# Transposing softmax tiles in 32x32 blocks on VectorE and placing the blocks by DMA over DRAM, in a two-layer attention trunk

## The chip, the cores and the metric

The kernel runs on one core of a Trainium2 chip. The metric is the device time of one execution in microseconds (us); 2468.92 us is the median of three runs of the kernel before (2468.75 to 2469.18). The trace was taken in one more execution on the same kind of chip.

## The reference

The reference is a two-layer encoder on 256 tokens of 2048 features, in float32. Each layer is a mixer and a gated feed-forward network (FFN, 5632 wide, with a convolution of width 3 on the gate), each behind an RMS norm and with a residual sum. Four kinds of attention heads make up the two mixers; in all of them a softmax over keys is multiplied with the values:

```python
# layer 0, A: 8 heads, three dilated windows each, merged by their softmax denominators
logits = einsum("bqhd,bqkhd->bhqk", qi, kg) * scale + rel_bias        # per (window, dilation)
o = einsum("bhqk,bqkhd->bqhd", exp(logits - m), vg) / denom
out_a = sum(softmax(stack(lses), axis=0)[..., None] * stack(outs), axis=0)
# layer 0, B: 4 heads, two softmax maps each
w = p[:, :, 0] - lam * p[:, :, 1];  o = einsum("bhqk,bkhd->bqhd", w, v)   # then a norm per head
# layer 1, C: 8 heads that share 2 key/value heads, with rotary q and k
o = einsum("bngqk,bknd->bqngd", softmax(logits), v)
# layer 1, D: 8 heads, a clamped 2-D neighbourhood with a learned bias
o = einsum("bhjrc,brjchd->bjhd", softmax(logits), vq)
```

Each mixer ends in an output projection of its concatenated heads. The output is the RMS norm of the last residual.

## The kernel before

Nearly all the work is projections, whose weights are read from DRAM once, in units of 128x1024 float32 (512 KB). For each unit SyncE starts a load into one of five `raw` buffers; ScalarE casts it to float32r (`wh`, line 230) and VectorE takes the rest (`wl = raw - wh`, line 233); there are four buffers of each. TensorE multiplies high by high, high by low and low by high parts. `gemm_b` (line 141) makes transposed results for queries, keys and the FFN: for two 128-wide results it runs four units' high products (line 132), then their low ones (line 138). `gemm_a` (line 198) makes row-wise results of 512 columns, a unit being 12 products (lines 194 to 196).

Attention work is put between the projections by a clock written out by hand. `tick()` (line 85) moves the clock on; `gemm_b` ticks twice (for queries and keys once between its high and low products and once behind them), `gemm_a` behind every second unit. `later(delay, fn, rank)` (line 81) queues a step for the tick `delay` ahead; in one tick steps of lower rank come first. `flush()` ticks until nothing is queued. The framework's planner then orders each engine's instructions by when it reckons them ready, except where `keep_in_program_order` pins one, and makes each wait only for what it needs and for its buffer to be released.

A head's steps are: queries and keys; two ticks later the logits (TensorE, then VectorE adds the bias into `sc` or `scc`) and the softmax (`softmax`, line 414, `b_softmax`, line 652, or `c_head`, line 818); two ticks later the transposes of the probabilities and their split into a high and a low part, `pt` (`transposed_probs`, line 393, `a_transposes`, line 570); then the products with the values: one tick later in A and B heads (`a_values`, `b_values`), two in C and D heads (`head_out`, line 402). B heads have one step more, `b_finish` (line 694). TensorE transposes 128x128 float32 blocks by a product with the identity, into PSUM tiles `tp` (`transpose_block`, line 273). An A head's softmax tile is 128x1024: per half of the queries 256 columns of the local window and 128 of each strided one. The other heads' tiles are 128x512. `sc` has one buffer; `scc` has two.

There are 28 heads: 8 A, 4 B, 8 C and 8 D. The A and B heads start one per three or two `gemm_b` calls, a C head one per tick, a D head one per `gemm_b`. `mixer_out` (line 326) is the output projection: it runs seven of eight units of its first two chunks with ticks, flushes, and then multiplies the last units, which need the last two head outputs (`mix`).

GpSimd does little: it loads bias rows (lines 538 and 545), runs of D's bias table (line 867) with a sum (line 871), and small constants, each through its own DMA queue.

Of the kernel before, what the change touches and what calls it, by code (L numbers as in the profile page):

```python
# [27 lines left out]
F32 = mybir.dt.float32  # L28
F32R = mybir.dt.float32r
AF = mybir.ActivationFunctionType  # L30
ALU = mybir.AluOpType
AX = mybir.AxisListType

P = 128
SEQ = 256
# [11 lines left out]
NACT = 24  # L47
RAW = 5
AHEAD = 4


def rev(ap):
# [6 lines left out]
def trunk_kernel(ctx: ExitStack, tc, a, out):  # L59
# [13 lines left out]
    def nm(s):  # L73
        uid[0] += 1
        return f"{s}_{uid[0]}"
# [5 lines left out]
    def later(delay, fn, rank=2):  # L81

        pending.append((now[0] + delay, rank, fn))
# [19 lines left out]
    def tps(tag, bufs):  # L103
        return psum.tile([P, 512], F32, name=nm(tag), tag=tag, bufs=bufs)
# [22 lines left out]
    def two(ap):  # L127
        return ap.rearrange("p (a b) -> p a b", a=2)
# [100 lines left out]
    def split(dst_h, dst_l, src, pin=False):  # L229
        first = S.copy(dst_h, src)  # L230
        if pin:
            tc.keep_in_program_order(first)
        V.tensor_tensor(dst_l, src, dst_h.bitcast(F32), op=ALU.subtract)  # L233
# [39 lines left out]
    def transpose_block(pairs):  # L273

        for i, (dst, src) in enumerate(pairs):
            ins = T.transpose(dst, src, ident)  # L276
            if i:
                tc.keep_in_program_order(ins)
# [90 lines left out]
    def logits(q, k):  # L369
        ps = two(tps("s", 2))  # L370
        for t in range(2):
            qh = q[:, 0, t * P:(t + 1) * P]
            ql = q[:, 1, t * P:(t + 1) * P]
            T.matmul(ps[:, t, :], qh, k[:, 0, :], start=True, stop=False)  # L374
            T.matmul(ps[:, t, :], qh, k[:, 1, :], start=False, stop=False)  # L375
            T.matmul(ps[:, t, :], ql, k[:, 0, :], start=False, stop=True)  # L376
        return ps

    def parity_bias(b):

        return bass.AP(tensor=b.tensor, offset=b.offset, ap=[list(b.ap[0]), [1, 2], [1, 2], [2, P]])

    def by_parity(ap):
        return ap.rearrange("p t (b a) -> p t b a", b=2)
# [5 lines left out]
    def new_pt():  # L390
        return att.tile([P, 2, 2, SEQ], F32R, name=nm("pt"), tag="pt", bufs=2)

    def transposed_probs(p0, p1, order=None):

        ps = two(tps("tp", 2))
        transpose_block([(ps[:, kt, t * P:(t + 1) * P], p[:, kt * P:(kt + 1) * P])
                         for kt in range(2) for t, p in enumerate((p0, p1))])
        pt = new_pt()
        split(pt[:, :, 0, :], pt[:, :, 1, :], order(ps) if order else ps)
        return pt  # L400

    def head_out(vt, cs, pt, slot):

        ps = tps("s", 2)[:, 0:SEQ]
        for kt in range(2):
            vh, vl = vt[kt]
            T.matmul(ps, vh[:, cs], pt[:, kt, 0, :], start=(kt == 0), stop=False)  # L407
            T.matmul(ps, vh[:, cs], pt[:, kt, 1, :], start=False, stop=False)  # L408
            T.matmul(ps, vl[:, cs], pt[:, kt, 0, :], start=False, stop=(kt == 1))  # L409
        o = new_act("mix", slot)  # L410
        split(o[:, 0, :], o[:, 1, :], ps)
        return o

    def softmax(sc, shared=False):

        mx = tmp.tile([P, 2], F32, name=nm("mx"), tag="mx")
        V.tensor_reduce(mx, sc, axis=AX.X, op=ALU.max)
        V.tensor_scalar(mx, mx, -1.0, None, op0=ALU.mult)
        den = tmp.tile([P, 2], F32, name=nm("den"), tag="den")
        for t in range(2):  # L420
            S.activation(sc[:, t, :], sc[:, t, :], AF.Exp, bias=mx[:, t:t + 1], accum_out=den[:, t:t + 1])
        V.reciprocal(den, den)
        for t in range(2):
            if shared and t == 0:
                S.activation(sc[:, t, :], sc[:, t, :], AF.Copy, scale=den[:, t:t + 1])
            else:
                V.tensor_scalar(sc[:, t, :], sc[:, t, :], den[:, t:t + 1], None, op0=ALU.mult)


    def x_load(u):  # L430
# [102 lines left out]
    def new_sc():  # L533
        return att.tile([P, 2, 512], F32, name=nm("sc"), tag="sc", bufs=1)
# [15 lines left out]
    def a_local(q, k, b, sc):  # L550
        sc.append(new_sc())
        sc = sc[0]
        V.tensor_tensor(by_parity(sc[:, :, 0:SEQ]), by_parity(logits(q, k)), parity_bias(b), op=ALU.add)

    def a_strided(g, q, k, b, sc):

        sc = sc[0]
        ps = tps("s", 2).rearrange("p (x t k) -> p x t k", x=2, t=2)
        for t in range(2):
            ks = slice((1 - t) * P, (2 - t) * P)  # L560
            ts = slice(t * P, (t + 1) * P)
            T.matmul(ps[:, :, t, :], q[:, 0, ts], k[:, :, ks], start=True, stop=False)  # L562
            T.matmul(ps[:, 1, t, :], q[:, 1, ts], k[:, 0, ks], start=False, stop=True)
        dst = sc[:, :, SEQ + (g - 1) * P:SEQ + g * P]
        V.tensor_tensor(dst, ps[:, 0, :, :], b.unsqueeze(1).to_broadcast([P, 2, P]), op=ALU.add)
        V.tensor_tensor(dst, dst, ps[:, 1, :, :], op=ALU.add)

    mix = [None] * KT

    def a_transposes(sc, hd, vg):  # L570
        pt = transposed_probs(sc[:, 0, 0:SEQ], sc[:, 1, 0:SEQ])
        ps = tps("tp", 2).rearrange("p (g t k) -> p g t k", g=2, t=2)
        for g in range(2):
            for t in range(2):
                T.transpose(ps[:, g, t, :], sc[:, t, SEQ + g * P:SEQ + (g + 1) * P], ident)
        pt4 = new_pt().rearrange("p g x (t k) -> p (g x t k)", t=2).rearrange("p (n x k) -> p n x k", x=2, k=P)
        split(pt4[:, :, 0, :], pt4[:, :, 1, :], ps.rearrange("p g t k -> p (g t) k"))
        later(1, lambda: a_values(hd, vg, pt, pt4), 0)

    def a_values(hd, vg, pt, pt4):  # L580
# [22 lines left out]
    def a_head(hd, vg):  # L603
        sc = []
        for g in range(3):
            b = a_bias(hd, g)
            q, k = qk_tiles([a["eva_qk"][hd * 6 + 2 * g + x] for x in range(2)], yT, (Rq, R), (rev, None), 2 * g)
            if g == 0:
                later(2, lambda q=q, k=k, b=b: a_local(q, k, b, sc))
            else:  # L610
                later(2, lambda g=g, q=q, k=k, b=b: a_strided(g, q, k, b, sc))

        def soft():
            softmax(sc[0])
            later(2, lambda: a_transposes(sc[0], hd, vg), 1)
        later(2, soft)

    for hh in range(2):
# [27 lines left out]
    def b_logits(m, q, k, sc, bias):  # L646
        if m == 0:
            sc.append(new_sc())
        V.tensor_tensor(by_parity(sc[0][:, :, m * SEQ:(m + 1) * SEQ]), by_parity(logits(q, k)), parity_bias(bias),
                        op=ALU.add)  # L650

    def b_softmax(hd, sc, vt):
        w = sc[0].rearrange("p t (m k) -> p t m k", m=2)
        mx = tmp.tile([P, 2, 2], F32, name=nm("mxb"), tag="mxb")
        V.tensor_reduce(mx, w, axis=AX.X, op=ALU.max)
        V.tensor_scalar(mx, mx, -1.0, None, op0=ALU.mult)
        den = tmp.tile([P, 2, 2], F32, name=nm("denb"), tag="denb")
        for t in range(2):
            for m in range(2):
                S.activation(w[:, t, m, :], w[:, t, m, :], AF.Exp, bias=mx[:, t, m:m + 1],  # L660
                             accum_out=den[:, t, m:m + 1])
        V.reciprocal(den, den)
        V.tensor_scalar(den[:, :, 1], den[:, :, 1], nlam, None, op0=ALU.mult)
        for t in range(2):
            V.tensor_scalar(w[:, t, 1, :], w[:, t, 1, :], den[:, t, 1:2], None, op0=ALU.mult)
            V.scalar_tensor_tensor(w[:, t, 0, :], w[:, t, 0, :], den[:, t, 0:1], w[:, t, 1, :],
                                   op0=ALU.mult, op1=ALU.add)
        later(2, lambda: b_transposes(hd, w, vt), 1)

    def b_transposes(hd, w, vt):  # L670
        pt = transposed_probs(w[:, 0, 0, :], w[:, 1, 0, :])
        later(1, lambda: b_values(hd, pt, vt), 0)

    def b_values(hd, pt, vt):
# [134 lines left out]
    def put(slot, tile_):  # L809
        mix[slot] = tile_  # L810

    def finish_head(sc, vt, cs, order, slot):
        def probs():
            pt = transposed_probs(sc[:, 0, :], sc[:, 1, :], order)
            later(2, lambda: put(slot, head_out(vt, cs, pt, slot)), 0)
        later(2, probs, 1)

    def c_head(q, k, vt, cs, slot):
        ps = logits(q, k)
# [13 lines left out]
    def d_head(hd, q, k, vt, y):  # L833
        ps = logits(q, k)
        sc = tmp.tile([P, 2, SEQ], F32, name=nm("scc"), tag="scc")
        V.tensor_tensor(sc, ps, bias_view(y.rearrange("p a b -> p (a b)"), P), op=ALU.add)
        softmax(sc, shared=True)
        finish_head(sc, vt, slice((hd % 4) * P, (hd % 4 + 1) * P), rev, 8 + hd)

    mix = [None] * KT  # L840
    ps = gemm_a(a["odc"][0], yT, KT, hooks={6: flush})
# [236 lines left out]
```

## Time and profile before

| | before |
|---|---|
| median of the runs | 2468.92 us |
| span of the profiled execution | 2467.0 us |
| TensorE busy | 2457.7 us (100%) |
| VectorE busy | 1605.3 us (65%) |
| ScalarE busy | 1262.6 us (51%) |
| GpSimd busy | 41.7 us (2%) |
| DMA of SyncE's queue | 454.52 MB, 56.8% of 16 engines |
| DMA of GpSimd's queue | 5.56 MB, 1.1% |

In the profile PE is TensorE's products, PEld its weight loads, DVE VectorE, ACT ScalarE and POOL GpSimd; SPq is SyncE's queue. A row of a group names line, engine, operation, output and input, the shapes, how often it came, its busy time in us and the mean length of one in ns, then the idle time of the engine ahead of it and what ended that. A row of a timeline gives the start in us from the start of the span, the length in us, and how many instructions are merged (x4). A matmul's length reaches into the next one, so its price is read from starts.

### The profile page before, as it was taken

The page shows a single profiled execution, that of the slowest core. Times are in us where ns is not written, and L with a number is a line of the kernel's source. Part 1 is how long each engine was busy: PE and PEld are TensorE (multiplying, and loading weights), DVE is VectorE, ACT ScalarE, POOL GpSimd, SP SyncE. Part 2 cuts the span into 40 slices and gives each one's busy share as a digit, 9 for nine tenths or more (in the row PEclk, how much of TensorE's full clock was granted, in tenths as well). Part 3 has the DMA queues.
Part 4 walks back from the last instruction along what each step waited for, and adds up shares of the span by engine and source line. Part 5 has one row for each costly group of instructions (what it writes and reads, how often), then busy time and mean ns, then how long its engine had stood idle before and what let it go on. Part 6 is the DMA issues. An engine that isn't in the chain of part 4 may idle for free.

```text
span 2467.0 us, 34369 instructions
## 1 busy us (share of the span) xinstructions
PE 2457.7 (100%) x13126; PEld 2127.5 (86%) x13126; DVE 1605.3 (65%) x2445; ACT 1262.6 (51%) x1876; POOL 41.7 (2%) x76
## 2 busy tenths in 40 slices
PE   9999999999999999999999999999999999999998
PEld 7888888888888888888888888888888888888887
DVE  6566567676667675476775567665667655676754
ACT  6555455465554543445444457555554533545443
POOL 1000000000000000000000000000000000000000
PEclk9999999999999999999999999999999999999999
DMA  8556555555555556655566555555555566555564
GB/s 309 183 169 194 172 178 186 172 181 191 179 179 186 190 190 202 189 185 191 190 196 194 188 180 156 177 180 179 176 192 190 186 204 192 184 188 189 191 202 146
DMA packets 129830, 462.93 MB, mean 188 GB/s; under 512 B 15224, under 2 KB 15480, under 8 KB 129664
## 3 DMA queue, kind: packets, MB, share of 16 engines
q1 hardware_dynamic: 126800, 454.52, 56.8%
q0 software_dynamic: 2432, 5.56, 1.1%
q8 instruction: 103, 1.69, 0.3%
q10 hardware_dynamic: 432, 0.66, 0.1%
q14 instruction: 63, 0.52, 0.1%
HBM read 458.48 MB, written 2.18 MB: 187 GB/s over the span
## 4 chain that ended last, share of the span: by engine, by line
PE 99%; DVE 0%; ACT 0%; issue 0%; DMA 0%; SPq 0%; DVEq 0%
PE gm L132 38%; PE gm L138 20%; PE gm L194 12%; PE gm L195 12%; PE gm L196 12%; PE tp L276 1%; PE s L375 0%; PE s L374 0%; PE s L376 0%; PE s L594 0%; PE s L562 0%; DMA raw<-in_eva_v 0%; PE s L409 0%; PE s L408 0%; PE s L407 0%
## 5 line engine op out<-in xcount | busy, mean ns | idle before, releaser
L233 DVE TENSOR_TENSOR wl<-raw,wh 128x1024 fp32r<-128x1024 f32 (+1 forms) x860 | 1035.3, 1216 | 622.2 <-ACT wh L230 366.1
L230 ACT CAST wh<-raw 128x1024 fp32r<-128x1024 f32 (+1 forms) x860 | 898.9, 1047 | 754.9 <-PE gm L196 428.8
L132 PE MATMUL gm<-yT,wh 128*128 128x512 f32 x4096 | 955.3, 390 | 0.0
L132 PEld LDWEIGHTS gm<-yT,wh 128*128 128x128 f32 x4096 | 760.5, 188 | 153.7 <-DVE yT L239 1.0
L138 PEld LDWEIGHTS gm<-yT,wl 128*128 128x128 f32 x4096 | 507.4, 192 | 9.1
L138 PE MATMUL gm<-yT,wl 128*128 128x256 f32 x4096 | 511.9, 283 | 0.0
L194 PE MATMUL gm<-wh,prod 128*128 128x512 f32 x702 | 273.4, 389 | 0.0
L195 PE MATMUL gm<-wl,prod 128*128 128x512 f32 x702 | 273.2, 389 | 0.0
L196 PE MATMUL gm<-wh,prod 128*128 128x512 f32 x702 | 273.1, 389 | 0.0
L223 ACT COPY t<-gm 128x256 f32<-128x256 f32 x256 | 95.6, 373 | 296.7 <-PE gm L138 296.7
L194 PE MATMUL gm<-wh,yT 128*128 128x512 f32 x412 | 161.0, 392 | 0.0
L195 PE MATMUL gm<-wl,yT 128*128 128x512 f32 x412 | 160.7, 390 | 0.1
L196 PE MATMUL gm<-wh,yT 128*128 128x512 f32 x412 | 160.7, 390 | 0.0
L196 PEld LDWEIGHTS gm<-wh,prod 128*128 128x128 f32 x702 | 131.8, 188 | 27.3
L195 PEld LDWEIGHTS gm<-wl,prod 128*128 128x128 f32 x702 | 131.8, 188 | 27.3
L194 PEld LDWEIGHTS gm<-wh,prod 128*128 128x128 f32 x702 | 131.8, 188 | 27.1
L224 DVE TENSOR_TENSOR t<-t,gm 128x256 f32<-128x256 f32 x256 | 105.6, 413 | 0.0
L194 PE MATMUL gm<-wh,mix 128*128 128x512 f32 x256 | 100.5, 393 | 0.0
L195 PE MATMUL gm<-wl,mix 128*128 128x512 f32 x256 | 99.8, 390 | 0.0
L196 PE MATMUL gm<-wh,mix 128*128 128x512 f32 x256 | 99.7, 390 | 0.0
L196 PEld LDWEIGHTS gm<-wh,yT 128*128 128x128 f32 x412 | 77.4, 188 | 16.2
L195 PEld LDWEIGHTS gm<-wl,yT 128*128 128x128 f32 x412 | 77.4, 188 | 15.9 <-DVE wl L233 0.5
(233 smaller groups left out, 1495.3 us busy)
## 6 DMA issues: line engine op xcount, KB each, us to landing
raw<-in_up SPq DMA_DIRECT2D x352, 512.0 KB, 4.2
raw<-in_down SPq DMA_DIRECT2D x176, 512.0 KB, 4.3
raw<-in_eva_qk SPq DMA_DIRECT2D x96, 512.0 KB, 4.0
raw<-in_eva_v SPq DMA_DIRECT2D x46, 512.0 KB, 4.5
raw<-in_evb_qk SPq DMA_DIRECT2D x32, 512.0 KB, 3.9
raw<-in_ev_out SPq DMA_DIRECT2D x32, 512.0 KB, 3.4
raw<-in_od_qk SPq DMA_DIRECT2D x32, 512.0 KB, 4.0
raw<-in_od_out SPq DMA_DIRECT2D x32, 512.0 KB, 3.4
```

What stands on the lines that cost most here:

```text
L132: T.matmul(ps.rearrange("p a b -> p (a b)"), wh[:, k * P:(k + 1) * P], act[u * 8 + k].rearrange("p a b -> p (a b)"), start=(u == 0 and k = ...
L138: T.matmul(ps[:, 1, :], wl[:, k * P:(k + 1) * P], act[u * 8 + k][:, 0, :], start=False, stop=(last and u * 8 + k == KT - 1))
L194: T.matmul(ps[t], ah, wh[:, sl], start=(kt == 0), stop=False)
L195: T.matmul(ps[t], ah, wl[:, sl], start=False, stop=False)
L196: T.matmul(ps[t], al, wh[:, sl], start=False, stop=(kt == nk - 1))
L223: S.copy(t0, ps[:, 0, :])
L224: V.tensor_tensor(t0, t0, ps[:, 1, :], op=ALU.add)
L230: first = S.copy(dst_h, src)
L233: V.tensor_tensor(dst_l, src, dst_h.bitcast(F32), op=ALU.subtract)
L276: ins = T.transpose(dst, src, ident)
```

## The change

In every head the softmax tile is transposed in place by VectorE (`V.transpose`), which turns each 32x32 block where it stands. Four DMAs from GpSimd's queue then store the tile, 32 rows each, to a DRAM tile `box`; in it the blocks lie so that four rows' groups come side by side. Four more DMAs per 512 columns (eight for an A tile) load `box` into an SBUF tile `pf`, 32 rows each, which then holds the full transpose. The split into `pt` reads `pf` in place of the PSUM tile. The split comes three ticks after the softmax, not two; in C and D heads the value products then follow one tick later, not two. `sc` is laid out anew, so that a tile's first half holds the 256 local columns of both query halves. For `pf` A and B heads take buffers of queries and keys (`qk4`, `qk5`); C and D heads take halves of `room`, an `sc` tile, and in slots 2, 3, 6 and 7 two activation buffers (`act22`, `act23`). D's reversed order is reversed in two dimensions (`rev2`).

```diff
-    def transposed_probs(p0, p1, order=None):
-
-        ps = two(tps("tp", 2))
-        transpose_block([(ps[:, kt, t * P:(t + 1) * P], p[:, kt * P:(kt + 1) * P])
-                         for kt in range(2) for t, p in enumerate((p0, p1))])
+    def turned(p, dsts):
+
+        n = p.shape[-1] // P
+        V.transpose(p, p)
+        box = dram.tile([32, n * 4, P], F32, name=nm("box"))
+        for i in range(4):
+            G.dma_start(box[:, :, i * 32:(i + 1) * 32],
+                        p[i * 32:(i + 1) * 32].rearrange("p (b c) -> p b c", c=32))
+        for x, dst in enumerate(dsts):
+            for j in range(4):
+                G.dma_start(dst[j * 32:(j + 1) * 32].rearrange("p a b -> p (a b)").rearrange("p (n q) -> p n q", q=P),
+                            box.rearrange("r (n j) q -> r j n q", j=4)[:, j, x * 4:(x + 1) * 4, :])
+
+    def new_turned(tag, pool=att):
+        return pool.tile([P, 2, SEQ], F32, name=nm("pf"), tag=tag, bufs=1)
+
+    def turned_probs(pf, order=None):
+
         pt = new_pt()
-        split(pt[:, :, 0, :], pt[:, :, 1, :], order(ps) if order else ps)
+        pv = pf.rearrange("p t (k q) -> p k t q", k=2)
+        pv = order(pv) if order else pv
+        pd = [pt[:, :, x, :].rearrange("p k (t q) -> p k t q", t=2) for x in range(2)]
+        split(pd[0], pd[1], pv)
         return pt
...
-    def a_transposes(sc, hd, vg):
-        pt = transposed_probs(sc[:, 0, 0:SEQ], sc[:, 1, 0:SEQ])
-        ps = tps("tp", 2).rearrange("p (g t k) -> p g t k", g=2, t=2)
-        for g in range(2):
-            for t in range(2):
-                T.transpose(ps[:, g, t, :], sc[:, t, SEQ + g * P:SEQ + (g + 1) * P], ident)
+    def a_transposes(pf, hd, vg):
+        pt = turned_probs(pf[0])
         pt4 = new_pt().rearrange("p g x (t k) -> p (g x t k)", t=2).rearrange("p (n x k) -> p n x k", x=2, k=P)
-        split(pt4[:, :, 0, :], pt4[:, :, 1, :], ps.rearrange("p g t k -> p (g t) k"))
+        split(*(pt4[:, :, x, :].rearrange("p (g t) k -> p g t k", g=2) for x in range(2)), pf[1].rearrange("p t (g k) -> p g t k", g=2))
         later(1, lambda: a_values(hd, vg, pt, pt4), 0)
...
         def soft():
-            softmax(sc[0])
-            later(2, lambda: a_transposes(sc[0], hd, vg), 1)
+            softmax(sc[0].rearrange("p x (t k) -> p t x k", t=2))
+            pf = [new_turned(f"qk{4 + x}") for x in range(2)]
+            turned(sc[0].rearrange("p a b -> p (a b)"), pf)
+            later(3, lambda: a_transposes(pf, hd, vg), 1)
         later(2, soft)
...
-        later(2, lambda: b_transposes(hd, w, vt), 1)
-
-    def b_transposes(hd, w, vt):
-        pt = transposed_probs(w[:, 0, 0, :], w[:, 1, 0, :])
+        pf = new_turned(f"qk{4 + hd % 2}")
+        turned(sc[0].rearrange("p m k -> p (m k)")[:, 0:512], [pf])
+        later(3, lambda: b_transposes(hd, pf, vt), 1)
+
+    def b_transposes(hd, pf, vt):
+        pt = turned_probs(pf)
         later(1, lambda: b_values(hd, pt, vt), 0)
...
+    room = new_sc()
+
     def finish_head(sc, vt, cs, order, slot):
+        pf = (room[:, slot % 2, :].rearrange("p (k q) -> p k q", k=2) if slot >= 8 or slot % 4 < 2
+              else new_turned(f"act{20 + slot % 4}", acts))
+        turned(sc.rearrange("p t k -> p (t k)"), [pf])
+
         def probs():
-            pt = transposed_probs(sc[:, 0, :], sc[:, 1, :], order)
-            later(2, lambda: put(slot, head_out(vt, cs, pt, slot)), 0)
-        later(2, probs, 1)
+            pt = turned_probs(pf, order)
+            later(1, lambda: put(slot, head_out(vt, cs, pt, slot)), 0)
+        later(3, probs, 1)
```

More of the change, by code (lines that the diff above doesn't have):

```diff
@@ L49, with rev2 @@
 AHEAD = 4
+def rev2(ap):
+    dims = [list(d) for d in ap.ap]
+    off = ap.offset
+    for x in (-1, -2):
+        st, n = dims[x]
+        off += st * (n - 1)
+        dims[x] = [-st, n]
+    return bass.AP(tensor=ap.tensor, offset=off, ap=dims)
 def rev(ap):
@@ L416, in softmax @@
         mx = tmp.tile([P, 2], F32, name=nm("mx"), tag="mx")
-        V.tensor_reduce(mx, sc, axis=AX.X, op=ALU.max)
+        V.tensor_reduce(mx, sc, axis=AX.X if len(sc.shape) == 3 else AX.XY, op=ALU.max)
         V.tensor_scalar(mx, mx, -1.0, None, op0=ALU.mult)
@@ L420, in softmax @@
         for t in range(2):
-            S.activation(sc[:, t, :], sc[:, t, :], AF.Exp, bias=mx[:, t:t + 1], accum_out=den[:, t:t + 1])
+            S.activation(sc[:, t], sc[:, t], AF.Exp, bias=mx[:, t:t + 1], accum_out=den[:, t:t + 1])
         V.reciprocal(den, den)
@@ L424, in softmax @@
             if shared and t == 0:
-                S.activation(sc[:, t, :], sc[:, t, :], AF.Copy, scale=den[:, t:t + 1])
+                S.activation(sc[:, t], sc[:, t], AF.Copy, scale=den[:, t:t + 1])
             else:
-                V.tensor_scalar(sc[:, t, :], sc[:, t, :], den[:, t:t + 1], None, op0=ALU.mult)
+                V.tensor_scalar(sc[:, t], sc[:, t], den[:, t:t + 1], None, op0=ALU.mult)
     def x_load(u):
@@ L552, in a_local @@
         sc = sc[0]
-        V.tensor_tensor(by_parity(sc[:, :, 0:SEQ]), by_parity(logits(q, k)), parity_bias(b), op=ALU.add)
+        V.tensor_tensor(by_parity(two(sc[:, 0, :])), by_parity(logits(q, k)), parity_bias(b), op=ALU.add)
     def a_strided(g, q, k, b, sc):
@@ L563, in a_strided @@
             T.matmul(ps[:, 1, t, :], q[:, 1, ts], k[:, 0, ks], start=False, stop=True)
-        dst = sc[:, :, SEQ + (g - 1) * P:SEQ + g * P]
+        dst = two(sc[:, 1, :])[:, :, (g - 1) * P:g * P]
         V.tensor_tensor(dst, ps[:, 0, :, :], b.unsqueeze(1).to_broadcast([P, 2, P]), op=ALU.add)
@@ L648, in b_logits @@
             sc.append(new_sc())
-        V.tensor_tensor(by_parity(sc[0][:, :, m * SEQ:(m + 1) * SEQ]), by_parity(logits(q, k)), parity_bias(bias),
+        V.tensor_tensor(by_parity(two(sc[0][:, m, :])), by_parity(logits(q, k)), parity_bias(bias),
                         op=ALU.add)
     def b_softmax(hd, sc, vt):
-        w = sc[0].rearrange("p t (m k) -> p t m k", m=2)
+        w = sc[0].rearrange("p m (t k) -> p t m k", t=2)
         mx = tmp.tile([P, 2, 2], F32, name=nm("mxb"), tag="mxb")
@@ L837, in d_head @@
         softmax(sc, shared=True)
-        finish_head(sc, vt, slice((hd % 4) * P, (hd % 4 + 1) * P), rev, 8 + hd)
+        finish_head(sc, vt, slice((hd % 4) * P, (hd % 4 + 1) * P), rev2, 8 + hd)
     mix = [None] * KT
```

## The prediction

> **What bounds the kernel now.** I read the page's busy table and its chain first, then the groups of instructions for the edited lines, then timelines around one head of each kind, the DMA view and the stretches by stage.
>
> ```profile
> span 2467.0 us, 34369 instructions
> ...
> PE 2457.7 (100%) x13126; PEld 2127.5 (86%) x13126; DVE 1605.3 (65%) x2445; ACT 1262.6 (51%) x1876; POOL 41.7 (2%) x76
> ...
> PE 99%; DVE 0%; ACT 0%; issue 0%; DMA 0%; SPq 0%; DVEq 0%
> ```
>
> TensorE (PE) works in 2457.7 of 2467.0 us and is 99% of the chain that ended last. So a TensorE instruction taken out is time taken out, unless something else then makes TensorE wait. The runs' median, 2468.92, is 1.9 us above this span, and I add that to everything below.
>
> **The transposes that go.** The groups of the transposes of probabilities, and the splits that follow them (after the bar: busy us, then mean ns):
>
> ```profile
> L233 DVE TENSOR_TENSOR pt<-tp,pt 128x512 fp32r<-128x512 f32 x36 | 23.9, 682 | 1.3 <-ACT pt L230 1.1
> L230 ACT CAST pt<-tp 128x512 fp32r<-128x512 f32 x36 | 20.4, 590 | 2.1 <-PE tp L276 1.4
> L276 PE MATMUL tp<-ident,scc 128*128 128x128 f32 x64 | 9.6, 272 | 0.0
> L276 PE MATMUL tp<-ident,sc 128*128 128x128 f32 x48 | 7.2, 272 | 0.0
> L575 PE MATMUL tp<-ident,sc 128*128 128x128 f32 x32 | 4.8, 273 | 0.0
> ```
>
> 64 + 48 + 32 = 144 transposes, 36 blocks of four. Their busy time is 21.6 us, but it overlaps what comes next, so I price a block by starts, on TensorE's timeline in an A head:
>
> ```profile
> 204.44 0.60 PE L276 MATMUL tp<-ident,sc 128*128 128x128 f32 x4
> 204.88 0.60 PE L575 MATMUL tp<-ident,sc 128*128 128x128 f32 x4
> 205.23 0.36 PE L374 MATMUL s<-qk,qk 128*128 128x256 f32 x1
> ```
>
> The second block starts 0.44 us after the first. 36 x 0.44 = 15.9 us, all on the path: the gain. 21.6 is no bound of it, since it counts the overlap with the next products. The 36 splits on ScalarE and VectorE stay, only their source moves from PSUM to SBUF; I cost that at nothing.
>
> **What VectorE adds.** 8 in-place block transposes of 128x1024 (A heads) and 20 of 128x512 (4 B, 8 C, 8 D). The trace has none; the nearest rows of VectorE over the same tiles are the scaling and the maximum:
>
> ```profile
> L417 DVE TENSOR_REDUCE mx<-sc 128x2 f32<-128x1024 f32 x8 | 9.7, 1212 | 0.1
> L427 DVE TENSOR_SCALAR sc<-sc,den 128x512 f32<-128x512 f32 x16 | 7.1, 483 | 0.2
> L417 DVE TENSOR_REDUCE mx<-scc 128x2 f32<-128x512 f32 x8 | 5.4, 678 | 0.1
> ```
>
> So 0.48 to 0.68 us for 512 columns, 0.97 to 1.21 for 1024: 17 to 23 us over 28 heads. I take 0.6 and 1.1, between the ends. The stretches of the C and the D heads show the room (after the length: busy us of PE, PEld, DVE, ACT, POOL; clock; DMA share):
>
> ```profile
> 1475.00:1535.00 60.00, 60.00 (x354) 53.09 (x353) 45.92 (x98) 45.70 (x104) 2.17 (x4) 1.00 0.48 151
> 1535.00:1665.00 130.00, 130.00 (x732) 114.17 (x731) 88.05 (x142) 71.37 (x127) 11.40 (x16) 1.00 0.56 178
> ```
>
> VectorE is busy 46 of 60 us and 88 of 130, so 8 x 0.6 = 4.8 us fits in each: nothing on the path. If that cover were gone (C, the tighter), it would cost those 4.8 us.
>
> **What the way over DRAM costs.** Each head now issues from GpSimd's queue 4 stores (a 512-column tile: 512 pieces of 128 B each; an A tile: 1024) and, after waiting for all four, 4 loads (A: 8) of 128 pieces of 512 B. Rows for issues and for issue to landing (last number, us):
>
> ```profile
> L545 POOL DMA_DIRECT2D bias<-rel x16 | 8.6, 536 | 159.0 <-DVE sc L565 158.8 <-issue 0.2
> L867 POOL DMA_DIRECT2D runs<-in_rpb x16 | 8.4, 527 | 2.1 <-POOL nb L871 2.1
> ```
> ```profile
> bias<-rel POOLq DMA_DIRECT2D x16, 64.0 KB, 4.1
> rel<-vals POOLq DMA_DIRECT2D x1, 56.0 KB, 1.8
> ```
>
> An issue takes 536 ns with 128 rows (bias) and 527 with 64 (runs): 9 ns for 64 more pieces, so about 0.6 us at 512 and 0.66 at 1024 if that slope holds; if all 536 ns grew with the pieces, 2.1 and 4.3 us. I take 0.54 to 0.6, because the two measured counts hardly differ, and keep the upper end for a rival. The Trainium skill (Perfetto Trace Analysis, DMA Instruction — SWDGE (GPSIMD)) says that such a record ends when the last GpSimd core has written its descriptors; by that rule the 9 ns are the whole price of 64 pieces, as I assume, and if the record were only a hand-over the generation would be unseen here.
>
> A store lands 1.8 us after its issue (rel<-vals), a load 4.1; I use 4.1 for both, the worse. Then an A head, from the end of its block transpose: 4 x 0.54 to the last store's end, 3.6 more to its landing, 8 x 0.54 for the loads, 3.6 more: 13.7 us. A 512-column head: 2.2 + 3.6 + 2.2 + 3.6 = 11.6.
>
> What time there is, in an A head:
>
> ```profile
> 193.27 7.50 PE L132 MATMUL gm<-yT,wh 128*128 128x512 f32 x32
> 200.61 4.00 PE L138 MATMUL gm<-yT,wl 128*128 128x256 f32 x32
> ```
> ```profile
> 198.72 0.88 DVE L427 TENSOR_SCALAR sc<-sc,den 128x512 f32<-128x512 f32 x2
> ...
> 201.76 2.36 DVE L233 TENSOR_TENSOR wl<-raw,wh 128x1024 fp32r<-128x1024 f32 x2 [1.83 <-PE gm L138]
> ...
> 207.04 0.68 DVE L553 TENSOR_TENSOR sc<-s,bias 128x512 f32<-128x512 f32 x1
> ```
>
> Softmax ends at 199.6, the transpose fits into the 1.83 us gap before 201.76, and the probabilities land at 201.0 + 13.7 = 214.7. Ticks alternate at 7.4 and 3.9 us; softmax belongs to that at 193.2, so its third is at about 212.5 (the splits) and its fourth at 216.4 (the value products). ScalarE, whose next weight casts queue behind the waiting split, may stand up to 2 us; TensorE is fed, since the two splits take 0.59 and 0.68 us each. The logits buffer, which the next head rewrites at 207.04, is free when the fourth store lands, 206.8. Behind the waiting loads in GpSimd's queue stand the next bias loads; with two buffers each has a whole projection, 11.3 us, until its use and needs 4.1 to land, so a wait of 3.6 costs nothing. Everything fits, barely. Of D and B heads (11.6 us from the transpose's end, softmax some 5 us) the same holds: 17.2 against a third tick at 18.7.
>
> C heads come faster:
>
> ```profile
> 1476.26 0.28 PE L374 MATMUL s<-cq,cq 128*128 128x256 f32 x1
> ...
> 1482.44 0.28 PE L374 MATMUL s<-cq,cq 128*128 128x256 f32 x1
> ```
>
> One every 6.2 us, while GpSimd, with loads held behind the landing, is taken 2.2 + 3.6 + 2.2 = 8.0 us per head: 8 x 1.8 = 14 us late at the end if its queue keeps heads apart; with stores landing in 1.8 us it takes 5.7 and nothing is late. I take 2 us, near the lower end, since the landing measured for a store is the short one and weights are cast ahead.
>
> **The steps that move by a tick.** Transposed probabilities come at the third tick, not the second. For A and B the value products follow one tick later than before, for C and D at the same tick. That bites only where work runs out: the last B head, whose output the projection waits for.
>
> ```profile
> 614.79 0.28 PE L683 MATMUL s<-v,pt 128*128 128x256 f32 x1
> ...
> 617.84 0.88 DVE L691 TENSOR_SCALAR ob<-s,rb_h 128x256 f32<-128x256 f32 x2
> ...
> 620.38 0.60 PE L276 MATMUL tp<-ident,ob 128*128 128x128 f32 x4
> ...
> 621.53 0.47 ACT L236 ACTIVATE mix<-tp,sub_gain 128x256 fp32r<-128x256 f32 x1
> ```
>
> From the last value product (615.1) to its normalised tile (618.7) is 3.6 us, then 0.44 for the transposes and about 0.9 to the first split: 5 us of chain. Two units cover it now. One tick later only one unit of 12 products stands between, 2.7 us: 2.3 us of idle TensorE. Bounds 0 (other units pulled ahead) to 4.5 (the second split waited for too); I take 2. The other place is the flush between the two halves of the A heads, where splits and value products come in two ticks back to back:
>
> ```profile
> 241.96 0.60 PE L575 MATMUL tp<-ident,sc 128*128 128x128 f32 x4
> 242.31 0.48 PE L194 MATMUL gm<-wh,yT 128*128 128x512 f32 x1
> ...
> 244.72 0.50 PE L585 MATMUL s<-pt,v 128*128 128x512 f32 x1
> ```
>
> Products of the next projection already stand between the transposes and the value products that the program puts right behind them, so the planner fills such holes: 1 us, bounds 0 and 11 (the head's DMA chain with no filling).
>
> **The sum.** -15.9 + 2 (C heads) + 2 (last B head) + 1 (flush) = -10.9 us: 2468.9 - 10.9 = 2458.0.
>
> **Rivals.** *All of it hidden:* the three small terms are nothing, 2468.9 - 15.9 = 2453. For it: one-tick slack and the filling just seen; against it: the A sum that only just closes.
>
> *Given back at the seams:* last B head 4.5, flush 3, C heads 8: 15.5, so 2468.5. For it: the C sum with 4.1 us landings; against: the store's 1.8.
>
> *DMA engines become the bound* (slower). Queue totals for 300 to 425 us (packets, MB, share of 16 engines):
>
> ```profile
> q1 hardware_dynamic: 5911, 21.51, 52.7%
> q0 software_dynamic: 528, 1.23, 4.8%
> ```
>
> GpSimd's queue took 0.048 x 16 x 125 / 1.23 = 78 engine-us per MB in pieces of 512 and 1028 B. At that price per byte a 512-column head (0.52 MB both ways) is 2.6 us of all 16 engines and fits. If a 128 B piece takes as long as a 512 B one, it is (1.05 + 0.26) x 78 / 16 = 6.4 us; the C stretch leaves 52% of 60 = 31 us, 8 heads want 51: 20 late. D heads have 44% of 11.5 = 5.1 us each, 1.3 x 8 = 10 late; A heads fit. 2458 + 30 = 2488. It decides from about 3.9 us per head (31/8). The Trainium skill (DMA: Bandwidth & Descriptors, Specifications) asks for at least 512 B per transfer for full rate and says that below it the engine reads, changes and writes back; no run here shows a 128 B store, and that rule speaks for this rival.
>
> *GpSimd's issue grows with the pieces* (slower): 4.3 us per A store makes the head's chain 28.7 us, 15 late, x 8 = 120; C heads hold the queue 14.4 us, 8 late, x 8 = 64; B and D about 1.3 x 12 = 15. 2458 + 199 = 2657. It decides where four A stores cost more than the 7.5 us block that could be put in between, so from about 2.4 us each.
>
> **How the numbers follow.** Forecast 0.35, all hidden 0.20, given back 0.17, DMA engines 0.13, issue cost 0.15. 0.2% is 4.9 us, about what a measurement of this kernel can tell from no change. Faster: 0.35 + 0.20 = 0.55; same 0.17; slower 0.28. The range runs from all hidden (2453, less 1 for the block's price) to the DMA rival's 2488 and a little, leaving out the 0.15 of the issue cost: 2452 to 2490.
>
> **What would show it.** Right: no transposes on sc or scc, TensorE busy down by 16 us and its idle time up by about 5, GpSimd issues at 0.5 to 0.7 us, stores landing in 2 to 4. Wrong: splits (pt) waiting on DMA for several us in each head, issues of over 1 us, a DMA share near 1 in the C stretch, or logits waiting for the stores to release their buffer.

## The result, and the profile after

The changed kernel takes 2504.3 us (median of four runs, 2502.74 to 2505.82) against 2468.86 before: ratio 1.0143, 95% interval 1.013 to 1.0155. It is 35 us slower. The forecast was 2458 us, range 2452 to 2490: wrong in sign and outside the range.

The page of the changed kernel; the lines are the span, the busy table and the chain that ended last:

```profile
span 2504.0 us, 34673 instructions
...
PE 2465.0 (98%) x12982; PEld 2119.9 (85%) x12982; DVE 1630.8 (65%) x2473; ACT 1261.6 (50%) x1876; POOL 197.7 (8%) x332
...
PE 88%; DMA 4%; DVE 2%; POOL 2%; issue 2%; ACT 1%; SPq 0%; DVEq 0%; POOLq 0%; ACTq 0%
```

TensorE has the 144 transposes fewer (13126 to 12982), yet is busy 7.3 us longer, and idle for 39.0 us (2504.0 - 2465.0) where it was idle for 9.3. Being busy longer with less to do means that it ran slower. The clock view says so; before it said 0.999:

```profile
core 0: 2504.0 us, clock 0.992
```

0.007 of 2504 us is 17.5 us of full clock lost. With 29.7 us more idle time and 15.9 us of transposes saved that makes 31 us; the other 6 of the 37 us by which the span grew are not resolved (waits shorter than the overlap of two products don't show as idle time).

Where it happens is read from instructions that both kernels share. The transposes of the residual close each mixer (duration ns, then first and last start): before, then after.

```profile
L276 PE MATMUL tp<-ident,h x96: 270/272/273, 634.5 to 1733.1; 128*128 128x128 f32 x96
```
```profile
L286 PE MATMUL tp<-ident,h x96: 270/272/273, 671.5 to 1770.2; 128*128 128x128 f32 x96
```

37.0 us late at the end of the first mixer, 37.1 at the end of the second: all the loss is in the A and B heads, and the C and D heads, with 7 us of transposes less, gain nothing.

What TensorE waited for, longest totals (us, times, longest):

```profile
PE s L607 <- DVE pt L243: 10.7, 6, 3.1
PEld s L607 <- DVE pt L243: 6.5, 6, 2.7
PEld s L616 <- DVE pt L243: 6.4, 5, 2.4
PEld s L433 <- ACT pt L240: 6.3, 9, 1.9
```

Lines 607 and 616 are an A head's value products, 433 a C or D head's. They stand for the split of the transposed probabilities. No row of TensorE names a weight load.

One such A head step by step. GpSimd's queue, ScalarE, VectorE and TensorE in the changed kernel (start, length, what; in brackets the idle time before):

```profile
173.31 3.10 POOL L409 DMA_DIRECT2D box<-sc  x4 [8.16 <-DVE sc L406]
181.65 4.35 POOL L413 DMA_DIRECT2D pf<-box  x8 [5.23 <-PE gm L148]
```
```profile
191.36 0.62 ACT L240 CAST pt<-pf 128x512 fp32r<-128x512 f32 x1 [1.83 <-DMA bias<-rel]
192.47 0.62 ACT L240 CAST pt<-pf 128x512 fp32r<-128x512 f32 x1 [0.49 <-DMA pf<-box]
```
```profile
171.78 1.24 DVE L406 STREAM_TRANSPOSE sc<-sc 128x1024 f32<-128x1024 f32 x1
...
189.44 4.63 DVE L243 TENSOR_TENSOR wl<-raw,wh 128x1024 fp32r<-128x1024 f32 x4 [5.94 <-issue]
193.99 0.68 DVE L243 TENSOR_TENSOR pt<-pf,pt 128x512 fp32r<-128x512 f32 x1
196.62 0.42 DVE L591 TENSOR_TENSOR sc<-s,bias 128x256 f32<-128x256 f32 x1 [1.95 <-PE s L589]
197.08 0.42 DVE L592 TENSOR_TENSOR sc<-sc,s 128x256 f32<-128x256 f32 x1
197.42 0.68 DVE L243 TENSOR_TENSOR pt<-pf,pt 128x512 fp32r<-128x512 f32 x1
```
```profile
194.73 0.73 PE L607 MATMUL s<-pt,v 128*128 128x512 f32 x2 [2.50 <-DVE pt L243]
...
198.16 0.58 PE L616 MATMUL s<-pt,v 128*128 128x256 f32 x1 [1.57 <-DVE pt L243]
```

From the block transpose's end (173.0) to the second loaded tile (192.5) it takes 19.4 us: 3.1 for four stores, 5.2 until the loads start, 4.35 for eight loads, 6.5 until the last has landed. (The idle row before the loads names a product; by then that was long done, and what the loads need is the four stores' landing.) VectorE then has the first low split behind four weight remainders of the next products (189.44 to 194.07) and the second behind a sum (line 591) that itself waits for TensorE, and TensorE stands twice: 2.5 and 1.6 us. Had VectorE taken the splits when ScalarE was done (191.98 and 193.09), TensorE would here have stood for half a microsecond. So this head alone says that the queue is to blame. Another head, the last before 510 us, says the tile: the second cast waits 4.45 us for the transfer, and the product goes as soon as that split is done.

```profile
506.17 0.62 ACT L240 CAST pt<-pf 128x512 fp32r<-128x512 f32 x1 [4.45 <-DMA pf<-box]
```
```profile
507.57 0.58 PE L616 MATMUL s<-pt,v 128*128 128x256 f32 x1 [2.24 <-DVE pt L243]
```

The head near 274 says the queue again (ScalarE, VectorE, TensorE):

```profile
273.79 1.04 ACT L240 CAST wh<-raw 128x1024 fp32r<-128x1024 f32 x1 [1.66 <-PE gm L206]
274.75 0.61 ACT L240 CAST pt<-pf 128x512 fp32r<-128x512 f32 x1
```
```profile
276.01 0.68 DVE L243 TENSOR_TENSOR pt<-pf,pt 128x512 fp32r<-128x512 f32 x1
```
```profile
276.84 0.79 PE L607 MATMUL s<-pt,v 128*128 128x512 f32 x2 [3.09 <-DVE pt L243]
```

The trace has the last of this tile's four loads landed at 271.9, and TensorE wants the product at 273.75; but ScalarE, idle for 1.66 us, casts a weight first, and VectorE a weight remainder. Four A heads have such waits (near 192, 274, 422 and 502 us), seven in all and 14.7 us long. Taken from the landings, with 1.5 us from there to the product (506.07 to 507.57 in the head above), only some 3.5 us of them wait for the transfers, near 192 and 502; some 11 us pass with the tile there and its splits behind other work. Whether another order would have won these 11 us takes an experiment (e11, below). What follows the wait near 192 us, in stretches of 4 us (after the length: busy us of PE and its products, PEld, DVE, ACT, POOL, then clock, DMA share, GB/s):

```profile
182.00:186.00 4.00, 4.00 (x20) 3.29 (x19) 1.51 (x2) 2.11 (x2) 4.00 (x8) 1.00 1.01 277
186.00:190.00 4.00, 4.00 (x26) 3.61 (x25) 0.56 (x1) 2.11 (x2) 0.56 (x2) 1.00 1.04 256
190.00:194.00 4.00, 2.23 (x19) 2.02 (x17) 4.00 (x5) 1.24 (x2) 0.00 (x0) 1.00 0.83 208
194.00:198.00 4.00, 1.85 (x8) 1.58 (x8) 2.02 (x5) 0.00 (x0) 0.55 (x1) 0.67 0.87 313
198.00:202.00 4.00, 2.50 (x9) 2.28 (x10) 1.50 (x5) 1.18 (x4) 0.00 (x0) 0.50 0.26 87
202.00:206.00 4.00, 4.00 (x12) 3.11 (x10) 1.87 (x6) 1.56 (x4) 0.00 (x0) 0.55 0.00 0
```

After the wait the granted clock falls to 0.50, and TensorE, busy throughout 202 to 206, does 12 products where 182 to 186 has 20. The clock falls at about 195.4 (the 0.67 is the mean of 194 to 198), 0.6 us after the wait of 2.5 us and before that of 1.6, and stays low for 10.2 us. Each of the four heads has such a stretch, 34 us in all, which is 17 us of full clock lost on top of 19.6 us of waits there (those of the products behind the heads, 0.8 to 1.3 us each, with them): a wait is paid nearly twice. The Trainium skill (TensorE: Matmul & The Clock Gate, Why this matters for your kernels) warns of idle gaps of over some 3 us between bursts of products, after which the clock is halved. This trace agrees in kind, though not in the length: near 192 one gap of 2.5 us was enough. The DMA share of 1.01 and 1.04 while tiles are loaded beside weights is also new: before, stretches of 4 us between 120 and 240 us have at most 0.97.

### The profile page after: what moved, and what is told of

Read it like the earlier page. It is cut to its first block, busy times and chain, and to the rows that moved or that the text cites. A ratio compares the mean times of both kernels' runs of the same rounds, so it can differ in the third digit from the quotient of the medians.

```text
span 2504.0 us, 34673 instructions
## 1 busy us (share of the span) xinstructions
PE 2465.0 (98%) x12982; PEld 2119.9 (85%) x12982; DVE 1630.8 (65%) x2473; ACT 1261.6 (50%) x1876; POOL 197.7 (8%) x332
## 3 DMA queue, kind: packets, MB, share of 16 engines
q0 software_dynamic: 11136, 24.45, 4.6%
## 4 chain that ended last, share of the span: by engine, by line
PE 88%; DMA 4%; DVE 2%; POOL 2%; issue 2%; ACT 1%; SPq 0%; DVEq 0%; POOLq 0%; ACTq 0%
PE gm L142 34%; PE gm L148 17%; PE gm L204 11%; PE gm L206 11%; PE gm L205 11%; DMA box<-sc 1%; POOL pf L413 1%; DMA runs<-in_rpb 1%; DMA pf<-box 1%; DMA bias<-rel 1%; PE tp L286 1%; POOL box L409 1%; DVE wl L243 0%; POOL sc L413 0%; DMA box<-scc 0%
## 5 line engine op out<-in xcount | busy, mean ns | idle before, releaser
L142 PE MATMUL gm<-yT,wh 128*128 128x512 f32 x4096 | 966.1, 392 | 4.2 <-DVE t L234 4.2
L409 POOL DMA_DIRECT2D box<-scc x64 | 41.2, 657 | 923.4 <-DVE scc L406 908.6
```

What stands on the lines that cost most here:

```text
L142: T.matmul(ps.rearrange("p a b -> p (a b)"), wh[:, k * P:(k + 1) * P], act[u * 8 + k].rearrange("p a b -> p (a b)"), start=(u == 0 and k = ...
L409: G.dma_start(box[:, :, i * 32:(i + 1) * 32], p[i * 32:(i + 1) * 32].rearrange("p (b c) -> p b c", c=32))
```

## The experiments

The theory now, *late tiles*: an A head's tile comes later than its value products' tick, TensorE waits, and the clock doubles the price. Rivals: *transfers* (the added traffic delays weights), *alike* (every changed head loses the same), *VectorE's work*, and *planned order* (the splits stand too far back in VectorE's queue, whenever the tile comes). Ratios are to the kernel before, 2469.1 us.

| run | us | ratio (95% interval) |
|---|---|---|
| e1, no wait for the tiles | 2460.6 | 0.9966 (0.9953 to 0.9979) |
| e2, C and D heads alone | 2468.6 | 0.9998 (0.9988 to 1.0007) |
| e3, A and B heads alone | 2502.2 | one run |
| e4, one load per 512 columns | 2464.0 | 0.998 (0.997 to 0.9989) |
| e5, A splits at the fourth tick | 2470.0 | 1.0004 (0.9995 to 1.0013) |
| e6, e4 and the last B head by TensorE | 2463.3 | 0.998 (0.9971 to 0.9989) |
| e7, e6 and the C heads by TensorE | 2461.1 | 0.9968 (0.9956 to 0.998) |
| e8, e7 and A splits at the fourth tick | 2459.2 | 0.9961 (0.9949 to 0.9974) |
| e9, e1 without the DMAs | 2455.5 | 0.9945 (0.9931 to 0.9958) |
| e10, e8 and all B heads by TensorE | 2458.7 | 0.9958 (0.9945 to 0.9972) |
| e11, splits ahead in VectorE's queue | 2506.3 | 1.0154 (1.0137 to 1.0171) |

**e1, no wait for the tiles.** Everything is issued, but the splits read the residual `h`:

```diff
-        pv = pf.rearrange("p t (k q) -> p k t q", k=2)
+        pv = h[:, :, 0:SEQ].rearrange("p t (k q) -> p k t q", k=2)
```

> The block transposes on VectorE and all stores and loads stay, but the splits read columns of the residual tile instead of the loaded tile, so nothing waits for the DMA chain (the attention outputs are then not those of the reference). Late tiles (value products wait for the landed tile, and TensorE's clock halves after each wait): 2453 to 2458 us, TensorE idle under 3 us, no stretch at half clock but the last. Transfers (small pieces hold the DMA engines and weights come late): stays near 2500. VectorE's added work: above 2470.

Measured 2460.6 us: 43.7 us less than with the wait, so the waits for the split tiles (with the slow clock behind them) are the loss. The clock view gives 0.999. It is not the 2453 to 2458 of the theory: half of the 15.9 us is still missing, which e9 takes up.

**e2 and e3, half of the heads.** e2 has the code of before for A and B heads, e3 for C and D heads.

> Only the 16 C and D heads are changed; A and B heads are transposed by TensorE as before. Late tiles in A and B: 2464 to 2470 us, since the after trace lost and regained 7 us over the C and D heads. If every changed head loses alike (35.4 us over 28 heads, 1.3 us a head): 2489.

> Only the 8 A and 4 B heads are changed. Late tiles in A and B: 2500 to 2508 us, with the half-clock stretches at the same places. Alike in every head: 2484.

2468.6 and 2502.2 us: the loss is all in A and B, and *alike* falls. The C and D heads neither gain nor lose.

**e4, one load per 512 columns.** The blocks are laid out in DRAM so that a tile's 128 rows are contiguous runs of 2 KB:

```diff
-        box = dram.tile([32, n * 4, P], F32, name=nm("box"))
+        box = dram.tile([4, 32, n, P], F32, name=nm("box"))
...
-            for j in range(4):
-                G.dma_start(dst[j * 32:(j + 1) * 32].rearrange("p a b -> p (a b)").rearrange("p (n q) -> p n q", q=P),
-                            box.rearrange("r (n j) q -> r j n q", j=4)[:, j, x * 4:(x + 1) * 4, :])
+            G.dma_start(dst.rearrange("p a b -> p (a b)"),
+                        box[:, :, x * 4:(x + 1) * 4, :].rearrange("j r n q -> (j r) (n q)"))
```

> The DRAM tile is laid out so that a full 128-row tile is loaded by one DMA: an A head has 4 stores and 2 loads in place of 4 and 8, the others 4 and 1 in place of 4 and 4; the bytes and the store pieces stay. Late tiles: the A chain gets 6 x 0.55 = 3.3 us shorter, and waits of 2 to 4 us mostly go: 2465 to 2480. Transfers: 2495 to 2505, since the bytes stay. If it is only the order planned on VectorE (the low split behind four weight casts): about 2500.

2464.0 us: 40 us faster than the changed kernel and 5 faster than before, with the same bytes and store pieces. That is more than the theory asked for. GpSimd's queue in an A head, and landings (KB, us):

```profile
164.07 3.98 POOL L409 DMA_DIRECT2D box<-sc  x4 [6.54 <-DVE sc L406]
174.33 1.10 POOL L412 DMA_DIRECT2D pf<-box  x2 [6.28 <-issue]
```
```profile
pf<-box POOLq DMA_DIRECT2D x24, 256.0 KB, 3.2
box<-sc POOLq DMA_DIRECT2D x32, 128.0 KB, 5.7
```

In the changed kernel the like rows read:

```profile
pf<-box POOLq DMA_DIRECT2D x96, 64.0 KB, 5.1
box<-sc POOLq DMA_DIRECT2D x32, 128.0 KB, 5.1
```

The stores got no faster (3.98 us for four, 5.7 to land); the loads go from 4.35 us of issue and 5.1 to land to 1.10 and 3.2, about 5 us off a chain that missed its tick by a few (first store's issue to last landing: 14.0 us in this head, 19.1 near 192 in the changed kernel). No A head's value product is left among TensorE's waits:

```profile
PE s L432 <- ACT pt L240: 3.0, 2, 1.7
```

Line 432 is a D head's product, so what waits is left in the second mixer.

**e5, A splits one tick later, all 12 DMAs kept.**

```diff
-            pf = [new_turned(f"qk{4 + x}") for x in range(2)]
+            pf = [new_turned(f"act{20 + x}", acts) for x in range(2)]
-            later(3, lambda: a_transposes(pf, hd, vg), 1)
+            later(4, lambda: a_transposes(pf, hd, vg), 1)
```

> The changed kernel with all its 12 DMAs per A head, but the A heads' splits come at the fourth tick in place of the third, into four activation buffers of their own kind (two are used) so that no query or key buffer is held. Late tiles: the waits in A heads (some 38 us with the slow clock after them) go, B's end and the C and D heads stay: 2466 to 2476. Transfers: no change, about 2504. The planned order on VectorE alone: 2490 or more, since the same instructions stand in the same queue.

2470.0 us. With the same DMAs, and more time until the split, 34 us of the 35 come back: the A heads' split tiles were late by less than a tick. The buffers differ too; but the loads start no sooner behind the stores (5.4 to 6.8 us in e5, 5.1 to 7.5 in the changed kernel), and e4 gains its 40 us with the old buffers, so held buffers weren't what made the tiles late. What e5 still waits for stands at B heads and, in the second row, at C or D heads:

```profile
PE s L707 <- ACT pt L240: 3.2, 2, 2.0
PE s L433 <- ACT pt L240: 2.7, 3, 1.2
```

e4 and e5 both give VectorE another order of issue as well, since the order is planned from when operands are reckoned to be there. That leaves *planned order* open, and e11 is for it.

**e11, the splits ahead in VectorE's queue.** All DMAs, tiles and ticks are those of the changed kernel. The weight remainders of the fifth and later units after an A head's splits, and the next sums of line 591, may not be issued ahead of the two low splits:

```diff
+    def behind(fn, unit=9):
+        with tc.issue_after(last[-1].ins) if last and unit > 4 else ExitStack(): fn()
...
-            split(wh[:, sl], wl[:, sl], raw[:, sl], pin=between is not None)
+            made[0] += 1; behind(lambda: split(wh[:, sl], wl[:, sl], raw[:, sl], pin=between is not None), made[0])
...
-        V.tensor_tensor(dst, ps[:, 0, :, :], b.unsqueeze(1).to_broadcast([P, 2, P]), op=ALU.add)
+        behind(lambda: V.tensor_tensor(dst, ps[:, 0, :, :], b.unsqueeze(1).to_broadcast([P, 2, P]), op=ALU.add))
...
-        split(*(pt4[:, :, x, :].rearrange("p (g t) k -> p g t k", g=2) for x in range(2)), pf[1].rearrange("p t (g k) -> p g t k", g=2))
+        low = split(*(pt4[:, :, x, :].rearrange("p (g t) k -> p g t k", g=2) for x in range(2)), pf[1].rearrange("p t (g k) -> p g t k", g=2)); last.append(low); made[0] = 0
```

> The changed kernel with all of its DMAs, tiles and ticks, and only VectorE's order of issue altered: the weight remainders of the fifth and later units after an A head's splits, and the bias sums of the next head's strided part, may not be issued ahead of the two low splits of the transposed probabilities. Nothing waits for anything new but the queue. Planned order: the low splits stood behind work that the planner had put ahead of them. By the rows of the changed kernel the order can take away 1.9 and 1.6 us of waits near 192, 2.7 us near 422 and 1.9 us near 502, together 8 of some 15 us of waits at A heads; each counted twice for the clock that gives about 2487 us, and 2465 to 2475 if the rest goes with it (no second wait within the first one's time, so no slow clock). Late tiles: the splits wait for landings, not for their place, VectorE now stands in front of its weight remainders until the tile is there, and the time is 2498 us or more. Transfers: 2504, unchanged.

2506.3 us: nothing gained in all. The waits shrink as reckoned near 192 (2.5 and 1.6 us become 0.48 and none), near 422 (2.7 us become none) and near 502 (4.8 become 1.7). Then they come back elsewhere: A heads' value products wait 15.5 us in all, in the changed kernel 15.6. The head near 264 us in e11 (GpSimd, ScalarE, VectorE, TensorE):

```profile
257.93 3.10 POOL L409 DMA_DIRECT2D box<-sc  x4 [5.33 <-DVE sc L406]
264.90 4.36 POOL L413 DMA_DIRECT2D pf<-box  x8 [3.87 <-ACT wh L240]
```
```profile
268.95 0.62 ACT L240 CAST pt<-pf 128x512 fp32r<-128x512 f32 x1 [4.66 <-DMA pf<-box]
```
```profile
269.60 0.69 DVE L243 TENSOR_TENSOR pt<-pf,pt 128x512 fp32r<-128x512 f32 x1 [11.96 <-ACT pt L240]
```
```profile
263.04 0.61 PE L204 MATMUL gm<-wh,yT 128*128 128x512 f32 x2
270.44 1.19 PE L607 MATMUL s<-pt,v 128*128 128x512 f32 x2 [6.78 <-DVE pt L243]
```

TensorE wants the tile at 263.7, before the first load is issued; VectorE stands in front of it for 12 us and runs the split as soon as ScalarE is done. Here the tile is late. But the edit has a part in it: in the changed kernel TensorE had projection products until 273.8 at this place, while here it comes to the value products 10 us sooner, behind two products with `wh` in a row, and VectorE makes no weight remainders while it stands. And what now stands behind the split is missed later. From TensorE's waits in e11:

```profile
PE s L607 <- DVE pt L243: 13.6, 6, 6.8
...
PE gm L142 <- DVE t L234: 7.7, 4, 2.9
```

The second row is new: the next products wait for a PSUM tile that VectorE empties late, with weight remainders in between. So this edit gains nothing, because holding VectorE costs what it saves. It doesn't show what the splits' place costs by itself: by the landings that is some 11 of the 14.7 us of waits, and *planned order* stays open beside *late tiles*. What e4 and e5 show is that a chain that ends sooner, or a later tick, takes away both.

**e6 and e7, parts put back on TensorE.** e6 is e4 with the old transposes and the old tick for the last B head (`hd == 3`); e7 adds the old way for C heads (`slot < 8`).

```diff
+        if slot < 8:
+            def by_pe():
+                pt = transposed_probs(sc[:, 0, :], sc[:, 1, :], order)
+                later(2, lambda: put(slot, head_out(vt, cs, pt, slot)), 0)
+            later(2, by_pe, 1)
+            return
```

> e4 (one load per 512 columns) with the last B head alone transposed by TensorE at the second tick, as before. If the moved tick costs at the projection's start what e1 and e4 show there (2.4 to 2.9 us less the 0.44 of its four transposes): 2461 to 2462, and no idle TensorE ahead of the transposes of that head's output. If that cost is something else: 2464.

> e6 with the 8 C heads also transposed by TensorE as before (D, A and three B heads by VectorE and DMA). Late tiles or late weights in the C stretch, where a head comes every tick, cost about what its 3.5 us of transposes bring: within 1.5 us of e6. If C heads gain as A heads do: 3.5 us slower than e6.

e6, 2463.3 us, is within the intervals of e4. In e4 TensorE is idle for 0.56 us twice around the last transposes of B's end, and in e6 it is not; but the first mixer ends no sooner (its first transpose of the residual at 631.4 us, in e4 at 631.1). The moved tick at B's end costs nothing that shows. e7, 2461.1, is not slower than e6 but by its median 2.2 faster, just within the intervals: C heads that come every tick don't repay the way over DRAM.

**e8 and e10, what the experiments point to.** e8 is e7 with e5's edit; e10 has all B heads on TensorE too, so that A and D heads alone go over DRAM.

> e7 with the A heads' splits at the fourth tick and in buffers of their own. Late tiles: A heads no longer wait at all, 1 to 2 us faster than e7, 2457 to 2461. If A heads have no waits left in e7: the same as e7.

> e8 with all four B heads transposed by TensorE: only A and D heads go over DRAM. The three B heads still changed in e8 save 1.3 us of transposes and show 0.8 us of wait: within 1 us of e8, 2458 to 2460. If changed B heads hold up more than that wait: 1 to 2 us faster than e8.

2459.2 and 2458.7 us, 9.8 and 10.3 us faster than before, and the same as each other within their intervals. Both beat both kernels. TensorE in e8:

```profile
PE 2447.6 (100%) x13018; PEld 2117.2 (86%) x13018; DVE 1624.6 (66%) x2464; ACT 1261.5 (51%) x1876; POOL 121.4 (5%) x179
```

Busy 10.1 us less than before: 108 transposes (27 blocks, e8 keeps 9) at 0.11 us would be 11.9.

**e9, e1 without the DMAs.** `turned` keeps only `V.transpose(p, p)`.

> e1 without its stores and loads: VectorE still turns the blocks, the splits read columns of the residual tile, nothing goes over DRAM (the attention outputs are not those of the reference). What the DMAs alone cost, waits for them apart, is the difference to e1 (2460.6). If the idle TensorE that e1 still shows in the C stretch (1.1 and 1.2 us, while weight casts wait for loads) comes from the transfers: 2457 to 2458. If it comes from the new ticks or from VectorE: the same as e1, 2460 to 2461.

2455.5 us, 5.2 less than e1. So the DMAs cost 5 us by being there, even when nobody waits for a tile. The C stretch in e9, then in e1 (same columns as above):

```profile
1475.00:1535.00 60.00, 60.00 (x350) 53.09 (x348) 51.12 (x108) 43.45 (x95) 4.28 (x7) 1.00 0.50 165
```
```profile
1475.00:1535.00 60.00, 57.59 (x322) 49.65 (x321) 49.19 (x101) 41.98 (x89) 30.27 (x51) 1.00 0.72 199
```

With the DMAs the share is 0.72 instead of 0.50 and TensorE is idle for 2.4 us (60.00 - 57.59). A wait there in e1, on ScalarE and then on TensorE:

```profile
1506.91 1.05 ACT L240 CAST wh<-raw 128x1024 fp32r<-128x1024 f32 x1 [1.83 <-DMA raw<-in_od_qk]
1507.87 0.37 ACT L240 CAST mix<-s 128x256 fp32r<-128x256 f32 x1
```
```profile
1508.74 0.39 PE L384 MATMUL s<-cq,cq 128*128 128x256 f32 x1 [1.12 <-DVE mix L243]
```

A cast waits 1.83 us for a weight, the mixed tile's cast stands behind it, and TensorE waits for that tile. In e9 the like cast waits too, 1.68 us, and TensorE doesn't; so whether it is the later weight or another order on ScalarE stays open. Of the difference 1.2 us is there at the end of the first mixer, and 4.8 more at that of the second. *Transfers* was thus a real term, but of 5 us, not of 40. And e9's 13.6 us of gain, with VectorE's block transposes all in place, is 2.3 short of the 15.9: if that price is right, it bounds *VectorE's work* and the moved ticks together.

## Why the prediction was wrong

- **The gain, 15.9 us.** Right: e9 has 13.6 of it with the moved ticks still in.
- **VectorE at nothing.** Right. The block transposes took 705 ns (512 columns) and 1.24 us (the 1024 above), a little over the upper bounds of 0.68 and 1.21, and stayed covered.
- **The DMA chain of an A head, "13.7 us ... Everything fits, barely".** This is the step that failed. It measured 19.4 us in the head shown:

| part | predicted | measured |
|---|---|---|
| 4 stores | 2.2 | 3.1 |
| until the loads start | 3.6 | 5.2 |
| 8 loads | 4.3 | 4.35 |
| to their landing | 3.6 | 6.5 |

The issue was nearly right (0.78 us for a store of 1024 pieces, 554 ns for a load). The landings were not: I took the 4.1 us of a single bias load in a quiet queue for transfers that come eight at a time beside weights, at a DMA share over 1. I also set the sum against the tick as if the two splits ran when the tile landed ("TensorE is fed, since the two splits take 0.59 and 0.68 us each"); they stood behind weight casts and remainders, which by the landings is some 11 of the 14.7 us of waits. A chain that "fits, barely" by medians needed a bound; its upper end by landings and queues, a few us late per head, was not in any of my cases.
- **What a wait costs.** The second failure: I priced a wait at its length. The clock fell to 0.50 after a wait of 2.5 us, and in the four heads that nearly doubled the price (17 us on 19.6). The trace of before could not show that, since TensorE hardly idled there; for that reason the price of a wait should have been left open upwards.
- **The other slower rivals.** *DMA engines* was small: without the DMAs e9 is 5 us faster than e1, most of it in the second mixer, and whether the engines' load does it is not shown; its upper price per 128 B piece did not come true. *Issue cost* was wrong: 657 ns at 512 pieces against 536 at 128 is 0.3 ns a piece, not 4.
- **Seams.** C heads taken at 2 us and B's end at 2 us: the C and D heads lost 7 us of their 7 (e2: no gain), more than I gave them; B's end costs two times 0.56 us of idle time in e4, and nothing that e6 shows in the total. The flush, taken at 1 us, was one of the places with waits in the changed kernel; in e4, e8 and e10 it has none.

- **Planned order**, no rival of mine, is the larger part of the waits near 192, 274 and 422 us; putting it right by holding VectorE (e11) gained nothing, and whether another way would is not shown.

Open: why some A heads wait and others don't, in the changed kernel four of eight for over 2 us in all (near 192, 274, 422 and 502 us); probably each wait moves the next head's products against its transfers, so that it changes from kernel to kernel. Open too is how the loss would part between landings and the splits' place in the queues if one could be changed alone, and what the 5 us of the DMAs are lost to.

## What to carry to other kernels

When a step leaves the bounding engine and takes a longer way round, put the way's length, with landings taken under the load that it will itself make and with the queues of the engines that take up its result, against the tick that uses it, and give it slack: here one tick more (e5) or six DMAs fewer per A head (e4) were each worth 34 to 40 us, and a better place in the queue, bought by holding VectorE (e11), nothing. On TensorE, price waits of 2 to 3 us at up to twice their length: the clock fell after most of them here. Change only the heads that have time: in e10 (one load per 512 columns) the mixers end 6.6 and then 10.1 us sooner than before, so A heads gained 6.6 and D heads 3.5, while putting the C heads back (e7) lost nothing.

## What was not expected of the hardware

- TensorE's granted clock fell to 0.50 for 10.2 us after a single wait of 2.5 us (near 192, the changed kernel) and for 3.4 us after one of 1.96 (near 614, e5). One of 2.15 us (near 651, the changed kernel) and single ones of up to 1.7 in e4 left it at 1.00. So the length of a wait alone didn't decide it.
- 128 B pieces were cheap: GpSimd's queue took 4.6% of 16 engines for 24.45 MB in the changed kernel,

```profile
q0 software_dynamic: 11136, 24.45, 4.6%
```

that is 0.046 x 16 x 2504 / 24.45 = 75 engine-us per MB, for stores in 128 B pieces and loads in 512 B pieces together, where before pieces of 512 and 1028 B took 78. The pieces aren't seen singly: 11136 packets for 24.45 MB are 2.2 KB each on the mean.
- A 128 KB store in 128 B pieces took 5.1 to 5.7 us to land where a 56 KB store in long rows took 1.8; a load of 256 KB in 2 KB rows landed in 3.2 us, one of 64 KB in 512 B pieces in 5.1, though these went out eight in a row and shared the engines.
